# A delta-rule chain with paired outputs, per-head increments, one masked scan and a column moved to ScalarE

## The chip, the cores and the metric

The program runs on one core of a Trainium2 chip. TensorE (PE) multiplies matrices, with its weight loads shown apart (PEld); VectorE (DVE), ScalarE (ACT) and GpSimd (POOL) work on tiles; SyncE (SP) issues the DMAs. Each engine takes its instructions in the order of its own queue and waits where an operand is not ready. The metric is the device time of one execution in microseconds, smaller being better.

## The reference

A decoder block on a sequence of 2048 tokens of width 1024 with two token mixers side by side, a convolution branch and an RWKV-7 branch. What the change touches is the second:

```python
    decay = jnp.exp(-jnp.exp(-jax.nn.softplus(-w_pre) - 0.5))
    ...
    def step(state, inp):
        r_t, w_t, k_t, v_t, kk_t, b_t = inp
        sk = jnp.einsum('bhvk,bhk->bhv', state, kk_t)
        state = (state * w_t[:, :, None, :] - sk[..., None] * b_t[:, :, None, :]
                 + v_t[..., None] * k_t[:, :, None, :])
        return state, jnp.einsum('bhvk,bhk->bhv', state, r_t)
```

There are 16 heads with a state of 64 by 64 each. Ahead of it, `_token_shift(z, mu)` forms `z + mu * (prev - z)` with the preceding token's row for `r`, `k`, `v` and two low-rank inputs. Around it stand one input projection from 1024 to 9344 columns, two branch output projections, a final projection and norms. Everything is computed in float32 accuracy: the projections split each operand into two reduced parts (`hi`, `lo`) and add three products.

## The kernel before

The sequence is cut into four blocks of 512 tokens (`TB`), and a block into eight chunks of 64 (`CH`, `NCH`). Features lie on the partitions. A block's input projection is a series of tiles of 128 features (`project`, `mm3`): eight feature tiles times three products, 24 matmuls of 512 columns at L179. While these run, the scheduler places between them the steps of generators that work on the recurrence: the generator's `yield a, b` says that the step takes about `a` us of TensorE and that the next is due `b` us later on a virtual clock, which each projection step moves on (`tick`, `poll`). The queues' final order comes from a scheduler that knows priorities; `tc.high_priority(HP)` lifts what is in it, and the convolution's taps (L890, 29 a tile plus a first and a last one, on VectorE) have a low one, so that they fill VectorE's queue.

**Token shift.** `shifted` (L466 to L474) gets a projection tile in PSUM. ScalarE forms `t1 = (1 - mu) * ps` (L468), VectorE adds `mu` times the columns one to the left for columns 1 to 511 (L470), then does the first column from the saved last column of the block before (`carry`, L472), then saves the new last column (L474). There are 25 such tiles a block.

**Pairs.** `pair` prepares two heads (128 features) of a block: 32 pairs in all. It makes the log-decay `M` by a tanh (L516), adds one to each column and sums along each chunk with eight scans of 64 columns (L524, `initial=0`, `one` the added ones), takes exponentials of the sums (L527, L529), and from `k` and `r` the tiles `BK` and `KR`; squares of `k` are summed over a head at L551, the chunk matrices come from `KR` and `BK` at L587, `tk` are transposes of `BK` (L607).

**Groups.** `group` takes two pairs (four heads) of a block: 16 groups, one after the other. It inverts the chunk matrices (POOL L671 and L673, PE L718 and L722) and then runs the chain over the eight chunks with the state `Sg` (two pairs `q`, two heads `hh` each, one head on partitions 0 to 63 and the other on 64 to 127). Two PSUM buffers `xo[0]` and `xo[1]` serve even and odd chunks. One chunk `c`, with `e = c % 2`:

- L775: state times `KR` into `xo[e][:, 0:2]`; ScalarE makes `Se` from the state (L779), VectorE `Xz` (L780).
- L784: the corrected values, on the half of `xo[e]`'s partitions that `prow(e)` names. Between its matmuls, one by one, stand those of the next chunk, L749, into the other buffer and the other half. After them come the outputs of the chunk before (`olast(c - 1)`, L758: four products of 64 columns on the half `vrow`). ScalarE copies `Xz` for the next chunk (L753) and the outputs (`ocopy`, L762); VectorE scales the values into `uv` (L795).
- L800: the state's increment, `tk` times `uv`, for both heads of a pair in one product of 128 by 128 of which the two diagonal blocks are used, into `xo[e][:, 2:4]`. VectorE updates the state in four instructions, one a head (L804).

After the last chunk come its outputs alone, then a group norm, and 30 us later on the virtual clock the transposes at L839. An fp32 matmul stands in the profile as two instructions. Tiles of PSUM come round from pools; a write into `xo` waits for what still reads or writes that buffer.

Of the kernel before, what the change touches and what calls it, by code (L numbers as in the profile page):

```python
# [9 lines left out]
F32 = mybir.dt.float32  # L10
F32R = mybir.dt.float32r
I32 = mybir.dt.int32
AF = mybir.ActivationFunctionType
ALU = mybir.AluOpType
# [4 lines left out]
P = 128  # L19
D = 1024  # L20
KT = D // P
TB = 512
NTT = TB // P
CH = 64
NCH = TB // CH
# [5 lines left out]
BKB, T2B, OCB = 1, 2, 2  # L31
KRB, TKB, ASB = 4, 4, 4
HP = 3000
# [33 lines left out]
def hybrid_block(ctx: ExitStack, tc: tile.TileContext, x, vecs, convk, w2a2, final_g, ada, w_in, w_co, w_ro, w_o, crow, out,  # L67
                 seq=2048, groups=(0, 1, 2, 3), phase2=True, dbg=None):
    nc = tc.nc
# [199 lines left out]
    c1 = late.enter_context(tc.tile_pool(name="c1", bufs=1))  # L269
    l3 = late.enter_context(tc.tile_pool(name="l3", bufs=3))  # L270
    lt = late.enter_context(tc.tile_pool(name="lt", bufs=2))
# [18 lines left out]
    nc.vector.tensor_scalar(out=hlb, in0=vc("conv_ln_b"), scalar1=0.5, scalar2=None, op0=ALU.mult)  # L290

    bones = c1.tile([P, P], F32R, name="bones")
    bf = lt.tile([P, P], F32, name="bf", tag="X", bufs=1)
    nc.vector.memset(bf, 0.0)
    nc.vector.memset(bf[0:64, 0:64], 1.0)
    nc.vector.memset(bf[64:128, 64:128], 1.0)
# [7 lines left out]

    Xz = c1.tile([P, 2, 2, P], F32, name="Xz")
    nc.gpsimd.memset(Xz, 0.0)
    one = c1.tile([P, CH], F32, name="one")
    nc.vector.memset(one, 1.0)
    maskA = c1.tile([P, 4, CH], F32, name="maskA")
    m64 = lt.tile([64, 2, CH], F32, name="m64", tag="X", bufs=1)  # L310
    nc.gpsimd.memset(m64, 1.0)
    for i, base in ((0, 0), (1, -1)):
        nc.gpsimd.affine_select(out=m64[:, i, :], in_=m64[:, i, :], compare_op=ALU.is_ge, fill=0.0, base=base,
# [10 lines left out]
    mu1 = dcol("mu1", "rwkv_mu", -1.0, 1.0)  # L324
# [13 lines left out]
    carry = c1.tile([P, 25], F32, name="carry")  # L338
# [126 lines left out]
    def shifted(ps, ti, dst):  # L465
        mi = ti - T_R  # L466
        t1 = e2.tile([P, TB], F32, name="t1", tag="t2", bufs=T2B)
        nc.scalar.activation(t1, ps, AF.Identity, scale=mu1[:, mi:mi + 1])  # L468
        mu = vc("rwkv_mu", mi)
        nc.vector.scalar_tensor_tensor(out=dst[:, 1:], in0=ps[:, 0:TB - 1], scalar=mu, in1=t1[:, 1:],  # L470
                                       op0=ALU.mult, op1=ALU.add)
        nc.vector.scalar_tensor_tensor(out=dst[:, 0:1], in0=carry[:, mi:mi + 1], scalar=mu, in1=t1[:, 0:1],  # L472
                                       op0=ALU.mult, op1=ALU.add)
        lastv[0] = nc.vector.tensor_copy(carry[:, mi:mi + 1], ps[:, TB - 1:TB])  # L474

    def ch3(ap):
        return ap.rearrange("p (c t) -> p c t", t=CH)
# [10 lines left out]
    def vrow(e):  # L488
        return slice(0, 64) if e == 0 else slice(64, 128)

    kcol, rcol = prow, vrow
# [9 lines left out]
    def pair(G, q_, box):  # L501
        b, pr, lora, uv, Asb, rn = G.b, 2 * G.g + q_, G.lora, G.uv, G.As[q_], G.rn
# [12 lines left out]
        M = e1.tile([P, TB], F32, name="M", tag="M")  # L515
# [3 lines left out]
        nc.tensor.matmul(pq, wlo[:, 1, :], lora[1], start=False, stop=True)  # L519
        ta = e1.tile([P, TB], F32, name="ta", tag="ta", bufs=1)  # L520
        nc.scalar.activation(ta, pq, AF.Tanh, scale=0.5, bias=a0h[:, pr:pr + 1])
        for c in range(NCH):
            cs = slice(c * CH, c * CH + CH)
            nc.vector.tensor_tensor_scan(out=M[:, cs], data0=one, data1=M[:, cs], initial=0.0, op0=ALU.add, op1=ALU.add)  # L524
        E1 = e1.tile([P, NCH, CH + 1], F32, name="E1", tag="E1", bufs=1)
        nc.gpsimd.memset(E1[:, :, 0:1], 1.0)
        nc.scalar.activation(E1[:, :, 1:], ch3(M), AF.Exp, scale=-DECAY)  # L527
# [16 lines left out]
        for e in range(2):  # L544
            nc.vector.scalar_tensor_tensor(out=KR[:, :, CH * (1 + e):CH * (2 + e)], in0=k4[:, :, e, :],
                                           scalar=vc("rwkv_k_k", pr), in1=E1x[:, :, e, :], op0=ALU.mult, op1=ALU.mult)
# [3 lines left out]
        for c in range(NCH):  # L550
            nc.tensor.matmul(pss[prow(c % 2), c // 2, :], sq[:, c * CH:c * CH + CH], hones, start=True, stop=True,  # L551
                             skip_group_check=True)
# [6 lines left out]
                                       scalar=hkk[:, pr:pr + 1], in1=E2.rearrange("p (c n) -> p c n", n=2 * CH),  # L559
                                       op0=ALU.mult, op1=ALU.mult)  # L560
# [18 lines left out]
        for c4 in range(NCH // 4):  # L579
            yield free  # L580
            pA = [pa.tile([P, 2, 256], F32, name="aux", tag="aux") for _ in range(2)]
            for c in range(4):
                cc, e = (c4 * 4 + c) // 2, c % 2
                es = slice(e * 128, e * 128 + 128)
                for hh in range(2):
                    hs = slice(64 * hh, 64 * hh + 64)
                    nc.tensor.matmul(pA[hh][:, c // 2, es], BK[hs, cc, es], KR[hs, cc, es],  # L587
                                     start=(c == 0), stop=(c == 3), skip_group_check=True)
            for hh in range(2):
                nc.vector.tensor_tensor(  # L590
                    out=Asb[:, hh, c4 * 4:c4 * 4 + 4, :].rearrange("p (a e) n -> p a (e n)", e=2),
                    in0=pA[hh], in1=flat(maskA).unsqueeze(1).broadcast_to([P, 2, 256]), op=ALU.mult)
# [8 lines left out]
        tk = l3.tile([P, NCH, P], F32, name="tk", tag="tk", bufs=TKB)  # L601
        for c4 in range(NCH // 4):
            yield free
            pt = pa.tile([P, 4, P], F32, name="aux", tag="aux")
            for c in range(4):
                cc, e = (c4 * 4 + c) // 2, c % 2
# [36 lines left out]
    lastv = [None]  # L643

    def group(G, before):
# [94 lines left out]
        O = uv[:, 0::2]  # L740
# [12 lines left out]
            nc.scalar.copy(Xz[prow(c % 2), c % 2], xo[c % 2][prow(c % 2), 2:4])  # L753

        def olast(c):
            vr, rc = vrow(c % 2), rcol(c % 2)
            for n, (q, hh, hs) in enumerate(every):
                nc.tensor.matmul(xo[c % 2][vr, q, hs], As[q][:, hh, c, rc], uv[:, c, q, hs],  # L758
                                 start=False, stop=(n == 3), skip_group_check=True)

        def ocopy(c):
            nc.scalar.copy(O[vrow(c % 2), c // 2], xo[c % 2][vrow(c % 2), 0:2])  # L762

        for n in range(4):
            xval(0, n)
# [3 lines left out]
        for c in range(NCH):  # L769
            cc, e = c // 2, c % 2  # L770
            pr_, b_ = prow(e), xo[e]
            es = slice(e * 128, e * 128 + 128)
            Se = lt.tile([P, 2, P], F32, name="Se", tag="Se", bufs=1)
            for q in range(2):
                nc.tensor.matmul(b_[:, q, :], R[q]["KR"][:, cc, es], Sg[:, q, :], start=(q == 0), stop=False,  # L775
                                 skip_group_check=True)
            with tc.high_priority(HP):
                for q in range(2):
                    nc.scalar.mul(Se[:, q, :], Sg[:, q, :], R[q]["pe"][:, c:c + 1])  # L779
                nc.vector.tensor_tensor(out=Xz[pr_, e], in0=b_[pr_, 0:2], in1=Xz[pr_, e], op=ALU.add)  # L780
            yield 0.6, 2.6

            for n, (q, hh, hs) in enumerate(every):
                nc.tensor.matmul(b_[pr_, q, hs], As[q][:, hh, c, kcol(e)], Xz[:, e, q, hs],  # L784
                                 start=(n == 0), stop=(n == 3), skip_group_check=True)
                if c + 1 < NCH:
                    xval(c + 1, n)
            if c:
                olast(c - 1)
            with tc.high_priority(HP):  # L790
                if c + 1 < NCH:
                    xcopy(c + 1)
                if c:
                    ocopy(c - 1)
                nc.vector.tensor_tensor(out=uv[pr_, c].rearrange("p q (h n) -> p q h n", n=64),  # L795
                                        in0=b_[pr_, 0:2].rearrange("p q (h n) -> p q h n", n=64),
                                        in1=rn[pr_, :, cc, :].unsqueeze(3).broadcast_to([64, 2, 2, 64]), op=ALU.mult)
            yield 1.1, 2.5
            for q in range(2):
                nc.tensor.matmul(b_[:, 2 + q, :], R[q]["tk"][:, c, :], uv[:, c, q, :], start=False, stop=(q == 1),  # L800
                                 skip_group_check=True)
            with tc.high_priority(HP):
                for q, hh, hs in every:
                    nc.vector.scalar_tensor_tensor(out=Sg[hs, q, hs], in0=b_[hs, 2 + q, hs],  # L804
                                                   scalar=R[q]["pe"][hs, c:c + 1], in1=Se[hs, q, hs],
                                                   op0=ALU.mult, op1=ALU.add)
            yield 0.6, 3.3
        olast(NCH - 1)
        ocopy(NCH - 1)

        O16 = O.rearrange("p a q (h n) -> p a (q h) n", n=64)
        st = lt.tile([P, 16], F32, name="gst", tag="gst")
# [505 lines left out]
```

## Time and profile before

| | us |
|---|---|
| median of 3 runs | 3033.8 (3033.46 to 3036.6) |
| the profiled execution | 3034.01 |
| its span, first to last instruction | 3032.2 |
| TensorE clock granted, mean share | 0.969 |

How the span divides: until 60 us the first tiles and the input norm are prepared; the four blocks' projections with the chain between them last until about 2440, and the last group's chain until about 2560 beside the output projections, which end the program. In these stretches TensorE's busy share and the others' are:

| us | PE | DVE | ACT | POOL |
|---|---|---|---|---|
| 60 to 760 | 634.45 | 524.85 | 274.77 | 333.48 |
| 760 to 1360 | 556.98 | 434.83 | 203.79 | 289.22 |
| 1360 to 1960 | 567.57 | 437.24 | 197.61 | 307.56 |
| 1960 to 2440 | 459.05 | 348.77 | 147.55 | 234.31 |

In the views below, a row of the timeline is start in us, length in us, engine, line, operation, tiles, shape and count; its length is from start to modelled end, and since matmuls overlap in the array, the distance of starts says what one costs. A row of the waits is who waited, for whom, total us, times, longest. A row of the groups by line gives busy time, mean ns of one instruction, and the idle time of the engine ahead of it.

### The profile page before, as it was taken

How to read it: one execution, taken by the hardware profiler on the slowest of the kernel's cores; microseconds unless marked ns; L12 is line 12 of the kernel's file. 1: busy time of each engine (PE TensorE's matmuls, PEld its weight loads, DVE VectorE, ACT ScalarE, POOL GpSimd, SP SyncE). 2: the span in 40 equal slices, each digit the busy share in tenths (PEclk: the TensorE clock that was granted, in tenths of full speed). 3: DMA queues.
4: the chain of work that ended last, by engine and by line, in shares of the span. 5: the costliest groups of instructions: out<-in, count | busy, mean ns of one | idle time of the engine just before them, and what ended most of it. 6: DMA issues, size and time to landing. Idle time of an engine off the chain costs nothing. (4 is left out here: it accounts for less than half of the span.)

```text
span 3032.2 us, 51026 instructions
## 1 busy us (share of the span) xinstructions
PE 2817.1 (93%) x18640; PEld 2297.6 (76%) x18640; DVE 2072.0 (68%) x4160; ACT 1001.3 (33%) x1936; POOL 1229.8 (41%) x1790
## 2 busy tenths in 40 slices
PE   6889798999799999999999999999999999899998
PEld 5767686777687777777878777778787778788988
DVE  6867777779676778676767777666778755753433
ACT  4424343434233324242423242323323323421211
POOL 3464637352536355425373655253644500400000
PEclk9989899999899999999999999999999999999999
DMA  8677657686757666857676668565656666976665
GB/s 309 234 247 249 217 204 257 204 268 197 241 187 258 198 203 218 284 173 240 191 257 203 210 217 305 168 208 171 193 184 213 237 210 195 336 250 222 215 222 174
DMA packets 363146, 680.00 MB, mean 224 GB/s; under 512 B 135632, under 2 KB 154384, under 8 KB 362896
## 3 DMA queue, kind: packets, MB, share of 16 engines
q1 hardware_dynamic: 362896, 676.75, 67.0%
q8 instruction: 147, 2.41, 0.3%
q14 instruction: 103, 0.84, 0.1%
HBM read 494.08 MB, written 181.41 MB: 223 GB/s over the span
## 5 line engine op out<-in xcount | busy, mean ns | idle before, releaser
L179 PE MATMUL ps_main<-h_hi,w_hi 128*128 128x512 f32 x2304 | 970.6, 421 | 19.7 <-DMA w_hi<-kh_in 15.1
L179 PE MATMUL ps_main<-h_hi,w_lo 128*128 128x512 f32 x2304 | 918.6, 399 | 7.2 <-POOL w_lo L164 4.0
L179 PE MATMUL ps_main<-h_lo,w_hi 128*128 128x512 f32 x2304 | 915.4, 397 | 1.3 <-DVE h_lo L397 1.1
L890 DVE SCALAR_TENSOR_TENSOR acc<-u,ck,acc 128x512 f32<-128x512 f32 x928 | 696.7, 751 | 15.9
L179 PEld LDWEIGHTS ps_main<-h_hi,w_hi 128*128 128x128 f32 x2304 | 442.9, 192 | 115.5 <-issue 9.9
L179 PEld LDWEIGHTS ps_main<-h_hi,w_lo 128*128 128x128 f32 x2304 | 440.7, 191 | 114.4 <-POOL w_lo L164 6.2
L179 PEld LDWEIGHTS ps_main<-h_lo,w_hi 128*128 128x128 f32 x2304 | 443.6, 193 | 81.6 <-DVE h_lo L397 2.9
L804 DVE SCALAR_TENSOR_TENSOR S<-xo,pe,Se 64x64 f32<-64x64 f32 x512 | 144.5, 282 | 140.1 <-PE xo L800 130.5
L671 POOL TENSOR_TENSOR itmp<-La,TT 128x126 f32<-128x126 f32 (+22 forms) x496 | 179.8, 363 | 130.2 <-DMA La<-dA 85.2
L162 ACT CAST w_hi<-w_st 128x1024 fp32r<-128x1024 f32 x103 | 108.1, 1049 | 301.4 <-DMA w_st<-w_co_t 124.8
L673 POOL TENSOR_TENSOR TT<-TT,itmp 128x126 f32<-128x126 f32 (+22 forms) x496 | 191.3, 386 | 36.8
L164 POOL TENSOR_TENSOR w_lo<-w_st,w_hi 128x1024 fp32r<-128x1024 f32 x50 | 120.4, 2408 | 131.2 <-ACT w_hi L162 67.3
L779 ACT ACTIVATE Se<-S,pe 128x128 f32<-128x128 f32 x256 | 88.9, 394 | 169.5 <-DVE S L804 169.4
L164 DVE TENSOR_TENSOR w_lo<-w_st,w_hi 128x1024 fp32r<-128x1024 f32 x53 | 65.6, 1238 | 97.2 <-PE ps_main L179 54.8
L795 DVE TENSOR_TENSOR uv<-xo,rn 64x256 f32<-64x256 f32 x128 | 53.6, 419 | 111.4 <-PE xo L784 99.3
L784 PEld LDWEIGHTS xo<-Xz,As 128*64 128x64 f32 x1024 | 70.0, 138 | 68.8 <-DVE Xz L780 32.0
L753 ACT COPY Xz<-xo 64x256 f32<-64x256 f32 x128 | 47.0, 367 | 211.9 <-PE xo L758 141.7
L780 DVE TENSOR_TENSOR Xz<-xo,Xz 64x256 f32<-64x256 f32 x128 | 53.5, 418 | 86.0 <-PE xo L775 78.9
L845 POOL TENSOR_TENSOR oc<-oc,zt 128x512 f32<-128x512 f32 x64 | 81.7, 1285 | 66.6 <-ACT oc L841 39.6
L784 PE MATMUL xo<-Xz,As 128*64 128x64 f32 x1024 | 87.9, 230 | 20.9 <-DVE Xz L780 20.8
L590 DVE TENSOR_TENSOR As<-aux,maskA 128x512 f32<-128x512 f32 x128 | 83.0, 682 | 30.9 <-PE aux L587 30.4
L587 PE MATMUL aux<-KR,BK 64*128 64x128 f32 x1024 | 82.2, 291 | 17.8 <-DVE As L590 9.3
(299 smaller groups left out, 5493.7 us busy)
## 6 DMA issues: line engine op xcount, KB each, us to landing
w_hi<-kh_in SPq DMA_DIRECT2D x219, 512.0 KB, 4.2
w_lo<-kl_in SPq DMA_DIRECT2D x219, 512.0 KB, 5.3
w_st<-w_in_t SPq DMA_DIRECT2D x73, 512.0 KB, 4.5
kh_in<-w_hi SPq DMA_DIRECT2D x71, 512.0 KB, 2.9
kl_in<-w_lo SPq DMA_DIRECT2D x71, 512.0 KB, 3.6
lny<-y_d SPq DMA_DIRECT2D x72, 256.0 KB, 4.4
w_hi<-kh_ro SPq DMA_DIRECT2D x32, 512.0 KB, 3.9
w_lo<-kl_ro SPq DMA_DIRECT2D x32, 512.0 KB, 5.3
```

Of the source, the lines that this page charges most:

```text
L162: nc.scalar.copy(hi, st)
L164: lo_eng.tensor_tensor(out=lo, in0=st, in1=hi.bitcast(F32), op=ALU.subtract)
L179: nc.tensor.matmul(ps[:, qs], ww[:, k, :], aa[k][:, qs], start=(k == 0 and t == 0 and q == 0), stop=(k == KT - 1 and t == 2 and q == ms - ...
L587: nc.tensor.matmul(pA[hh][:, c // 2, es], BK[hs, cc, es], KR[hs, cc, es], start=(c == 0), stop=(c == 3), skip_group_check=True)
L590: nc.vector.tensor_tensor(out=Asb[:, hh, c4 * 4:c4 * 4 + 4, :].rearrange("p (a e) n -> p a (e n)", e=2), in0=pA[hh], in1=flat(maskA).unsqu ...
L671: nc.gpsimd.tensor_tensor(out=tmp[:, :ni, :nt], in0=La[:, j:j + 1, j + 1:].broadcast_to([P, ni, nt]), in1=TT[:, :ni, j:j + 1].broadcast_to ...
L673: nc.gpsimd.tensor_tensor(out=TT[:, :ni, j + 1:], in0=TT[:, :ni, j + 1:], in1=tmp[:, :ni, :nt], op=ALU.add)
L779: nc.scalar.mul(Se[:, q, :], Sg[:, q, :], R[q]["pe"][:, c:c + 1])
L784: nc.tensor.matmul(b_[pr_, q, hs], As[q][:, hh, c, kcol(e)], Xz[:, e, q, hs], start=(n == 0), stop=(n == 3), skip_group_check=True)
L804: nc.vector.scalar_tensor_tensor(out=Sg[hs, q, hs], in0=b_[hs, 2 + q, hs], scalar=R[q]["pe"][hs, c:c + 1], in1=Se[hs, q, hs], op0=ALU.mult ...
L845: nc.gpsimd.tensor_tensor(out=oc, in0=oc, in1=zt, op=op)
L890: nc.vector.scalar_tensor_tensor(out=acc if i + 1 < HALO else yj, in0=u[:, i:i + TB], scalar=ck[:, j, i:i + 1], in1=acc, op0=ALU.mult, op1 ...
```

## The change

Four edits, and two small tiles that move to another buffer.

- Outputs of two chunks by turns: `olast` is called once after each odd chunk, for that chunk and the one before, its matmuls alternating between `xo[0]` and `xo[1]`, and with it ScalarE's two copies. The step after the odd chunk's state update is due after 2.0 instead of 3.3, then comes the output step with 0.5 and 1.5.
- State increment per head by turns: four products of 64 by 64 columns instead of two of 128 by 128, into columns 0 to 63 of `xo[e][:, 2 + q]`, on the partitions of the head.
- Decay sums: ScalarE adds one to all of `M`, then one scan of 512 columns multiplies the running sum by `keep` (ones, and zero at each chunk's first column) and adds `M`.
- Token shift: ScalarE forms the first column from the projection's first column, with `carry` as bias, and the new `carry` as `mu` times the last column.

```diff
-    bf = lt.tile([P, P], F32, name="bf", tag="X", bufs=1)
+    bf = lt.tile([P, P], F32, name="bf", tag="oc", bufs=OCB)
...
-    one = c1.tile([P, CH], F32, name="one")
-    nc.vector.memset(one, 1.0)
+    one1 = c1.tile([P, 1], F32, name="one1")
+    nc.vector.memset(one1, 1.0)
+    keep = c1.tile([P, TB], F32, name="keep")
+    nc.vector.memset(keep, 1.0)
+    nc.vector.memset(keep[:, 0::CH], 0.0)
...
-    m64 = lt.tile([64, 2, CH], F32, name="m64", tag="X", bufs=1)
+    m64 = lt.tile([64, 2, CH], F32, name="m64", tag="oc", bufs=OCB)
...
-        nc.vector.scalar_tensor_tensor(out=dst[:, 1:], in0=ps[:, 0:TB - 1], scalar=mu, in1=t1[:, 1:],
+        nc.scalar.activation(dst[:, 0:1], ps[:, 0:1], AF.Identity, scale=mu1[:, mi:mi + 1], bias=carry[:, mi:mi + 1])
+        nc.scalar.activation(carry[:, mi:mi + 1], ps[:, TB - 1:TB], AF.Identity, scale=mu)
+        lastv[0] = nc.vector.scalar_tensor_tensor(out=dst[:, 1:], in0=ps[:, 0:TB - 1], scalar=mu, in1=t1[:, 1:],
                                        op0=ALU.mult, op1=ALU.add)
-        nc.vector.scalar_tensor_tensor(out=dst[:, 0:1], in0=carry[:, mi:mi + 1], scalar=mu, in1=t1[:, 0:1],
-                                       op0=ALU.mult, op1=ALU.add)
-        lastv[0] = nc.vector.tensor_copy(carry[:, mi:mi + 1], ps[:, TB - 1:TB])
...
-        for c in range(NCH):
-            cs = slice(c * CH, c * CH + CH)
-            nc.vector.tensor_tensor_scan(out=M[:, cs], data0=one, data1=M[:, cs], initial=0.0, op0=ALU.add, op1=ALU.add)
+        nc.scalar.activation(M, M, AF.Identity, bias=one1[:, 0:1])
+        nc.vector.tensor_tensor_scan(out=M, data0=keep, data1=M, initial=0.0, op0=ALU.mult, op1=ALU.add)
...
         def olast(c):
-            vr, rc = vrow(c % 2), rcol(c % 2)
             for n, (q, hh, hs) in enumerate(every):
-                nc.tensor.matmul(xo[c % 2][vr, q, hs], As[q][:, hh, c, rc], uv[:, c, q, hs],
-                                 start=False, stop=(n == 3), skip_group_check=True)
-
-        def ocopy(c):
-            nc.scalar.copy(O[vrow(c % 2), c // 2], xo[c % 2][vrow(c % 2), 0:2])
+                for e in range(2):
+                    nc.tensor.matmul(xo[e][vrow(e), q, hs], As[q][:, hh, c + e, rcol(e)], uv[:, c + e, q, hs],
+                                     start=False, stop=(n == 3), skip_group_check=True)
+            with tc.high_priority(HP):
+                for e in range(2):
+                    nc.scalar.copy(O[vrow(e), c // 2], xo[e][vrow(e), 0:2])
...
-            if c:
-                olast(c - 1)
...
-                if c:
-                    ocopy(c - 1)
...
-            for q in range(2):
-                nc.tensor.matmul(b_[:, 2 + q, :], R[q]["tk"][:, c, :], uv[:, c, q, :], start=False, stop=(q == 1),
-                                 skip_group_check=True)
+            for q, hh, hs in every:
+                nc.tensor.matmul(b_[hs, 2 + q, 0:64], R[q]["tk"][:, c, hs], uv[:, c, q, hs], start=False,
+                                 stop=(q + hh == 2), skip_group_check=True)
...
-                    nc.vector.scalar_tensor_tensor(out=Sg[hs, q, hs], in0=b_[hs, 2 + q, hs],
+                    nc.vector.scalar_tensor_tensor(out=Sg[hs, q, hs], in0=b_[hs, 2 + q, 0:64],
...
-            yield 0.6, 3.3
-        olast(NCH - 1)
-        ocopy(NCH - 1)
+            yield 0.6, 2.0 if e else 3.3
+            if e:
+                olast(c - 1)
+                yield 0.5, 1.5
```

In the changed kernel the lines are numbered L776 (was L775), L781 (L780), L785 (L784), L750 (L749), L759 (L758), L792 (L795), L797 (L800), L801 (L804), L525 (L524).

## The prediction, made before the changed kernel ran

> **What bounds the kernel now.** I read the page first, then the list of who waits for whom on TensorE, then the timeline of TensorE around single visits of the chain.
>
> ```profile
> span 3032.2 us, 51026 instructions
> ...
> PE 2817.1 (93%) x18640; PEld 2297.6 (76%) x18640; DVE 2072.0 (68%) x4160; ACT 1001.3 (33%) x1936; POOL 1229.8 (41%) x1790
> ```
>
> TensorE is busy for 93% of the span and no other engine comes near it. So the end moves by two things alone: time in which TensorE's queue is occupied, and time in which the instruction at its head waits. The chain itself is not the bound: between its steps the queue holds 9 to 15 projection matmuls (L179), and a step that gets longer costs nothing while they cover it. The waits of the chain (L775 to L804) and of the pair work that feeds it (L551, L587, L718, L722) are these:
>
> ```profile
> PE xo L784 <- DVE Xz L780: 20.8, 14, 3.8
> ...
> PE aux L587 <- DVE As L590: 9.3, 7, 4.5
> PE late L722 <- DVE Qs L728: 9.1, 8, 1.9
> PE late L718 <- DVE T L705: 7.9, 2, 4.6
> PE aux L587 <- POOL KR L570: 7.8, 6, 2.8
> PE xo L758 <- DVE S L804: 7.5, 3, 4.4
> PE aux L551 <- ACT sq L543: 5.6, 3, 3.1
> ...
> PE xo L775 <- ACT Xz L753: 2.7, 2, 2.4
> ```
>
> Columns: total us, times, longest. Without L758 and the last row they come to 20.8 + 9.3 + 9.1 + 7.9 + 7.8 + 5.6 = 60.5 us, nearly all released by VectorE, directly or through what it feeds. That is what a lighter VectorE can give back.
>
> **What one visit of TensorE costs.** Projection matmuls start 0.23 us apart. A visit's price is the time from the last projection matmul before it to the second one after it, less two such steps (0.46).
>
> ```profile
> 282.41 0.40 PE L179 MATMUL ps_main<-h_hi,w_lo 128*128 128x512 f32 x1
> ...
> 283.25 0.63 PE L758 MATMUL xo<-uv,As 128*64 128x64 f32 x8
> ...
> 284.15 0.40 PE L179 MATMUL ps_main<-h_lo,w_hi 128*128 128x512 f32 x1
> ```
> ```profile
> 286.45 0.39 PE L179 MATMUL ps_main<-h_hi,w_lo 128*128 128x512 f32 x1
> 286.68 0.60 PE L800 MATMUL xo<-uv,tk 128*128 128x128 f32 x4
> ...
> 287.36 0.40 PE L179 MATMUL ps_main<-h_lo,w_hi 128*128 128x512 f32 x1
> ```
> ```profile
> 325.77 0.40 PE L179 MATMUL ps_main<-h_hi,w_lo 128*128 128x512 f32 x1
> 326.09 0.68 PE L758 MATMUL xo<-uv,As 128*64 128x64 f32 x8
> ...
> 327.04 0.39 PE L179 MATMUL ps_main<-h_lo,w_hi 128*128 128x512 f32 x1
> ```
> ```profile
> 372.39 0.40 PE L179 MATMUL ps_main<-h_hi,w_lo 128*128 128x512 f32 x1
> ...
> 372.94 0.22 PE L749 MATMUL xo<-uv,As 128*64 128x64 f32 x1
> ...
> 373.18 0.22 PE L749 MATMUL xo<-uv,As 128*64 128x64 f32 x1
> ...
> 373.67 0.40 PE L179 MATMUL ps_main<-h_lo,w_hi 128*128 128x512 f32 x1
> ```
>
> An fp32 matmul is two instructions here. In the same order: the mixed visit (16 of L784 and L749, then 8 of L758) costs 284.15 - 282.41 - 0.46 = 1.28 us; the increment L800 (4, of 128 columns) 0.45; the group's last outputs L758 alone (8) 0.81; 16 of L784 and L749 by turns 0.82. So 16 by turns cost what 8 on one half of the columns cost. And half of those 16 would save only 373.18 - 372.94 = 0.24, that is 0.58 us: most of a visit of 64-column tiles is a fixed price of entering and leaving, which the 128-column L800 does not pay.
>
> **Outputs by turns.** Each of the 16 groups now pays the mixed visit in seven of its eight steps, in the eighth with an L784 that has no L749 beside it (priced as 8 on one half, 0.81), and the last visit. The outputs' part is 6 x (1.28 - 0.82) + (1.28 - 0.81) + 0.81 = 4.04 us. After: four visits of 16 by turns, 4 x 0.82 = 3.28. Saved: 0.76 us a group, 12 us in all.
>
> **Increment per head.** Eight instructions of 64 columns in place of four of 128: 0.58 - 0.45 = 0.13 us more where the visit stands alone. In the built order 82 of the 128 do: +10.7 us. The other 46 stand beside transposes (L607), the KR-BK products (L587) or the like, and share one price of entering with them or pay a second one. The mixed visit shows the first (L758 behind L749 adds its 8 starts alone); if each shared all of it, they would save about as much as the 82 lose, if none, they add 6. I take nothing. Outputs and increments together: -12 + 11 = -1 us, with -10 to +5 as bounds. What is saved by turns goes back into entering and leaving more often.
>
> The Trainium skill, in TensorEngine Tiling, Key Properties, says that a change of tiling mode, not merely of tile, drains TensorE. The visits above agree (0.58 against 0.45). By that rule taken strictly, a neighbour of another tile size such as L587 would share nothing, and the two edits would come to about +5 rather than -1.
>
> **Scan.** Columns: busy us, mean ns, then idle time before.
>
> ```profile
> L890 DVE SCALAR_TENSOR_TENSOR acc<-u,ck,acc 128x512 f32<-128x512 f32 x928 | 696.7, 751 | 15.9
> L524 DVE TENSOR_TENSOR_SCAN M<-one,M 128x64 f32<-128x64 f32 x256 | 90.9, 420 | 8.4 <-ACT M L516 8.1
> L474 DVE COPY carry<-ps_main 128x1 f32<-128x1 f32 x96 | 14.4, 150 | 1.5
> L472 DVE SCALAR_TENSOR_TENSOR r<-carry,v,t 128x1 f32<-128x1 f32 x32 | 13.6, 424 | 0.0
> L472 DVE SCALAR_TENSOR_TENSOR vv<-carry,v,t 128x1 f32<-128x1 f32 x32 | 11.3, 353 | 0.0
> L472 DVE SCALAR_TENSOR_TENSOR k<-carry,v,t 128x1 f32<-128x1 f32 x32 | 10.0, 312 | 0.0
> L516 ACT ACTIVATE M<-aux,w0h 128x512 f32<-128x512 f32 x32 | 21.9, 685 | 7.7 <-PE aux L514 7.5
> L779 ACT ACTIVATE Se<-S,pe 128x128 f32<-128x128 f32 x256 | 88.9, 394 | 169.5 <-DVE S L804 169.4
> ```
> ```profile
> 240.88 1.95 DVE L524 TENSOR_TENSOR_SCAN M<-one,M 128x64 f32<-128x64 f32 x8
> ```
>
> A pair's eight scans hold VectorE for 90.9 / 32 = 2.8 us on the mean, 1.95 when nothing interferes. One scan of 512 columns is bounded by the plain 512-column tap below (0.75) and by the eight back to back above (1.95); I take 1.3, between. VectorE is spared 32 x (2.8 - 1.3) = 48 us. ScalarE gains 32 activations like L516, 22 us, and each pair's exponentials wait for it, so they start 2.8 - 1.3 - 0.7 = 0.8 us sooner.
>
> The Trainium skill, in DVE: opcode table, instruction layouts, handler registers and perf-mode slots, section 6, says that the built-in scan runs at half throughput because of its feedback; by that, 512 columns would cost about two taps, an estimate of 1.5 us, and the sum would change by 6 us of VectorE time alone.
>
> **First column.** L472 and L474 leave VectorE: 13.6 + 11.3 + 10.0 + 14.4 = 49 us. Two ScalarE instructions of one column take their place, 200 in all, each under L779's 0.39 us: at most 79 us on an engine that is busy a third of the time. They stand behind the activation that already reads the same projection; k, r and vv are ready 0.3 to 0.4 us sooner, since the column runs beside the 511-column instruction.
>
> So VectorE loses 48 + 49 = 97 of 2072 us. In the built order the usual number of taps (L890) ahead of a state update falls from four to three. Of the 60.5 us of waits I take a third back, 20 us: more than the tap in four, since the blocks of eight scans in the update's way go too. The bounds are nothing and half (30).
>
> **New waits.** The outputs of an odd step's two chunks are written into the buffer that this step's state update (L804, four instructions) is reading, so the visit waits for the update; behind it in TensorE's queue wait all projections. Before, only the last of a group's eight had this, behind 15 projection matmuls, and 3 of 16 were late, for 7.5 us together (quoted above). Now all 64 have it, behind 9: the cover shrinks by 6 x 0.23 = 1.4 us, so these three add 4. For the other 48, one odd step as it is now:
>
> ```profile
> 1027.92 0.60 PE L800 MATMUL xo<-uv,tk 128*128 128x128 f32 x4
> ```
> ```profile
> 1028.22 0.75 DVE L470 SCALAR_TENSOR_TENSOR k<-ps_main,v,t 128x511 f32<-128x511 f32 x1
> 1028.89 0.21 DVE L472 SCALAR_TENSOR_TENSOR k<-carry,v,t 128x1 f32<-128x1 f32 x1
> 1029.01 0.75 DVE L890 SCALAR_TENSOR_TENSOR acc<-u,ck,acc 128x512 f32<-128x512 f32 x1
> 1029.67 1.19 DVE L804 SCALAR_TENSOR_TENSOR S<-xo,pe,Se 64x64 f32<-64x64 f32 x4
> ```
>
> The update ends at 1030.86, 2.94 us after the increment's start; the new cover from there is about 0.24 + 0.15 + 8 x 0.23 + 0.32 = 2.5 us (the visit's own starts, the way out at 373.18 to 373.33, eight steps, the way in). Late by 0.45. Bounds for the 48: nothing, and 48 x 0.45 = 22. I take 5, since one such step has its L472 in front, which goes, and usually a tap fewer. Together +9, up to 26. Also, three times a group the next even step's L775 must wait for ScalarE's copy of these outputs, six projection matmuls earlier. The nearest row is L775 behind L753: 2.7 us in two waits, 1.35 each. I take 2, at most six such waits, 8.
>
> **Sum.** -1 + 9 + 2 - 20 = -10 us against the profiled execution's own 3034.0 (its span and 1.8 around it; the median of the runs is 3033.8): **3024 us**.
>
> **Rivals.**
> *Nothing moves.* VectorE's saved time falls into its idle third; a tenth of the waits comes back (6) and the new ones cost 6: about 3033. For it: many of these waits hang on a DMA or a weight split further back. Against: L784's wait for L780 is VectorE's own queue.
> *Slower: outputs behind the state update.* Place: the output visit of an odd step. It decides once these waits pass 19 us, where they eat the whole sum: 4 for the three late ones and 0.45 in 33 of the other 48. Price at the upper bound, with a third of the hoped return (7): 26 + 2 - 1 - 7 = +20, 3054. For it: the odd step above. Against: the scans that hold VectorE for 1.95 us in one piece become one shorter piece.
> *It doesn't do what it says.* L797's halves write one PSUM buffer, L784 and L749 two; were the turns not to overlap there, eight starts at L758's pace, 0.81 against 0.45 a visit, cost 0.36 x 82 = 30 us: 3054 with the other terms. Against it: L551, which writes one buffer with alternate halves, makes 16 starts in a visit like the one of L784 and L749:
>
> ```profile
> 730.25 0.40 PE L179 MATMUL ps_main<-h_hi,w_lo 128*128 128x512 f32 x1
> 730.57 0.63 PE L551 MATMUL aux<-bones,sq 128*64 128x2 f32 x16
> ...
> 731.48 0.39 PE L179 MATMUL ps_main<-h_lo,w_hi 128*128 128x512 f32 x1
> ```
>
> **How the numbers follow.** Forecast 0.46, nothing moves 0.19, outputs behind the update 0.28, no overlap 0.07. A difference under 0.2% (6 us) cannot be told from none. Faster 0.46, same 0.19, slower 0.35. The forecast's own range is 2999 (half the old waits back, the three late ones and a tenth of the 48 the only new ones: -1 + 6 - 30 = -25, and 10 for the visits' bound) to 3028. To hold 8 in 10 the range takes in both slower cases: 2999 to 3056.
>
> **What would show it.** A visit of eight L797 alone at 0.58 us, of 16 L759 at 0.82; L525 at 1.3 us; VectorE's busy time near 1975; L784's wait for Xz and L587's waits down by a third; L759's wait for S near 9 us. I am wrong if L759's waits pass 20 us, if L797's visits cost 0.8, or if the old waits stay although VectorE is lighter.

## The result and the profile after

The changed kernel takes 3042.0 us (median of 13 runs), the one before 3033.8 (13 runs): ratio 1.0028, 95% interval 1.0019 to 1.0037. It is slower by 8 us; 3024 had been forecast. The profiled executions have spans of 3039.8 and 3032.2.

The page of the changed kernel, first part:

```profile
span 3039.8 us, 51701 instructions
...
PE 2803.5 (92%) x19152; PEld 2237.3 (74%) x19152; DVE 2003.5 (66%) x3738; ACT 1066.8 (35%) x2168; POOL 1243.1 (41%) x1790
```

TensorE's span is its busy time and its idle time. Busy fell from 2817.1 to 2803.5, by 13.6 us; idle rose from 215.1 to 236.3, by 21.2. The difference is the 7.6 us by which the span grew: TensorE has less to do and waits longer. Where it waits, in the list of TensorE's waits (total us, times, longest):

```profile
PE xo L797 <- DVE uv L792: 16.3, 16, 2.8
PE ps_main L179 <- DVE mr L1142: 16.1, 4, 13.6
...
PE late L719 <- DVE T L706: 14.4, 4, 8.1
...
PE aux L588 <- POOL KR L571: 10.9, 7, 3.1
PE xo L785 <- DVE Xz L781: 10.7, 11, 1.6
PE xo L759 <- DVE S L801: 9.8, 8, 4.5
PE late L723 <- DVE Qs L729: 8.2, 5, 2.2
PE aux L719 <- DVE T L706: 8.1, 5, 3.6
...
PE aux L588 <- DVE As L591: 4.0, 4, 3.0
...
PE aux L552 <- ACT sq L544: 3.2, 1, 3.2
...
PE xo L776 <- ACT uv L763: 2.5, 3, 1.2
```

The same list of the kernel before, rows that the prediction does not show:

```profile
PE ps_main L179 <- DVE mr L1144: 9.8, 5, 6.5
...
PE aux L718 <- DVE T L705: 2.9, 3, 1.2
...
PE xo L800 <- DVE uv L795: 1.9, 3, 0.8
```

Two waits are new in size: the increment's wait for `uv` (16.3 for 1.9), and the projection matmuls' wait for `mr`, whose longest went from 6.5 to 13.6. The second is a single wait in one place. To find it, the span is cut at two projection matmuls that are the same in every kernel, the 7,393rd and the 7,585th L179: between them lies the work behind the last group (the last layer norm and the first projections behind it). The windows' columns are the stretch, its length, TensorE's busy time and count, granted clock, DMA share, GB/s. Before:

```profile
0.00:2607.20 2607.20, 2412.94 (x16335) 0.97 0.67 224
2607.20:2662.60 55.40, 47.31 (x195) 0.94 0.88 305
```

After:

```profile
0.00:2603.90 2603.90, 2397.87 (x16845) 0.97 0.67 223
2603.90:2670.40 66.50, 48.65 (x196) 0.85 0.80 283
```

Up to the last layer norm the change is 3.3 us ahead in these two executions: 15.1 less busy, 11.8 more idle. Then 11.1 us are lost in 66.5. In the timelines, columns as in the prediction's, the last entry is the idle time ahead and who ended it. TensorE, before:

```profile
2618.17 1.02 PE L1189 MATMUL pvar<-qs,ones 128*128 128x512 f32 x2
2625.73 0.79 PE L179 MATMUL ps_main<-m_hi,w_hi 128*128 128x512 f32 x1 [6.54 <-DVE mr L1144]
```

VectorE, before:

```profile
2624.40 0.68 DVE L1191 TENSOR_SCALAR ve<-pvar 128x512 f32<-128x512 f32 x1
2625.00 0.67 DVE L1144 SCALAR_TENSOR_TENSOR mr<-rth,ps_main 128x512 f32<-128x512 f32 x1
```

TensorE, after:

```profile
2618.95 2.07 PE L1187 MATMUL pvar<-qs,ones 128*128 128x512 f32 x2 [3.52 <-POOL qs L1185]
2634.64 0.79 PE L179 MATMUL ps_main<-m_hi,w_hi 128*128 128x512 f32 x1 [13.62 <-DVE mr L1142]
```

VectorE, after:

```profile
2622.86 5.38 DVE L1256 SCALAR_TENSOR_TENSOR xt<-xt,rs,fg 128x512 f32<-128x512 f32 x8
2628.16 0.68 DVE L1099 TENSOR_TENSOR o_lo<-zt,o_hi 128x512 fp32r<-128x512 f32 x1
2628.76 0.68 DVE L1189 TENSOR_SCALAR ve<-pvar 128x512 f32<-128x512 f32 x1
...
2632.70 1.28 DVE L1099 TENSOR_TENSOR o_lo<-zt,o_hi 128x512 fp32r<-128x512 f32 x2
2633.91 0.68 DVE L1142 SCALAR_TENSOR_TENSOR mr<-rth,ps_main 128x512 f32<-128x512 f32 x1
```

The rows of VectorE follow each other without idle time in both. It frees the PSUM buffer for which TensorE waits (`mr`) right behind `ve` before the change; after it, up to 0.6 us a piece, three steps of the reciprocal root and five splits of `o_lo` come between (rows left out above). Counted from the start of the second window, `pvar` starts 4.0 us later than before (3.5 of them a wait for `qs`), `ve` 7.6 and `mr` 12.1. Both orders compute the same; the queue was laid out anew, in a place that no line of the diff names.

### The profile page after: what moved, and what is told of

Its sections match the earlier page's. It is cut to its first block, busy times and chain, and to the rows that moved or that the text cites. A ratio compares the mean times of both kernels' runs of the same rounds, so it can differ in the third digit from the quotient of the medians.

```text
span 3039.8 us, 51701 instructions
## 1 busy us (share of the span) xinstructions
PE 2803.5 (92%) x19152; PEld 2237.3 (74%) x19152; DVE 2003.5 (66%) x3738; ACT 1066.8 (35%) x2168; POOL 1243.1 (41%) x1790
## 5 line engine op out<-in xcount | busy, mean ns | idle before, releaser
L179 PE MATMUL ps_main<-h_hi,w_hi 128*128 128x512 f32 x2304 | 971.9, 422 | 11.3 <-DMA w_hi<-kh_in 6.5
L179 PE MATMUL ps_main<-h_hi,w_lo 128*128 128x512 f32 x2304 | 917.8, 398 | 18.0 <-DMA w_lo<-kl_in 11.2
L179 PE MATMUL ps_main<-h_lo,w_hi 128*128 128x512 f32 x2304 | 912.4, 396 | 0.2
L179 PEld LDWEIGHTS ps_main<-h_hi,w_lo 128*128 128x128 f32 x2304 | 439.6, 191 | 126.0 <-DMA w_lo<-kl_in 13.8
L179 PEld LDWEIGHTS ps_main<-h_hi,w_hi 128*128 128x128 f32 x2304 | 440.9, 191 | 111.8 <-DMA w_hi<-kh_in 6.9
L179 PEld LDWEIGHTS ps_main<-h_lo,w_hi 128*128 128x128 f32 x2304 | 441.7, 192 | 78.6 <-DVE h_lo L400 1.1
L801 DVE SCALAR_TENSOR_TENSOR S<-xo,pe,Se 64x64 f32<-64x64 f32 x512 | 144.7, 283 | 142.9 <-PE xo L797 133.8
L781 DVE TENSOR_TENSOR Xz<-xo,Xz 64x256 f32<-64x256 f32 x128 | 53.7, 420 | 152.9 <-PE xo L776 148.2
L780 ACT ACTIVATE Se<-S,pe 128x128 f32<-128x128 f32 x256 | 88.9, 394 | 186.6 <-DVE S L801 183.8
L627 POOL TENSOR_TENSOR vv<-rk,vv 128x512 f32<-128x512 f32 x32 | 41.4, 1295 | 205.0 <-PE aux L624 154.0
L754 ACT COPY Xz<-xo 64x256 f32<-64x256 f32 x128 | 46.9, 366 | 202.9 <-PE xo L750 201.9
L792 DVE TENSOR_TENSOR uv<-xo,rn 64x256 f32<-64x256 f32 x128 | 53.8, 420 | 93.4 <-PE xo L750 59.0
L785 PEld LDWEIGHTS xo<-Xz,As 128*64 128x64 f32 x1024 | 69.2, 137 | 57.5 <-issue 30.5
L588 PE MATMUL aux<-KR,BK 64*128 64x128 f32 x1024 | 82.0, 295 | 16.9 <-POOL KR L571 10.9
```

Of the source, the lines that this page charges most:

```text
L179: nc.tensor.matmul(ps[:, qs], ww[:, k, :], aa[k][:, qs], start=(k == 0 and t == 0 and q == 0), stop=(k == KT - 1 and t == 2 and q == ms - ...
```

## The experiments

Each kernel ran in rounds with the kernel before; a ratio is to that, with its 95% interval. "Stretch" and "tail" are the two windows above, read from the one execution that was profiled. e3 and e12 are the same kernel, and their stretches are 12 us apart, TensorE's busy time 8 us (2806.9 and 2814.8): a stretch carries that much scatter, while the tail is 55.4 in both. So the ratios decide, and a stretch only hints.

| label | edits in it | ratio | stretch | tail |
|---|---|---|---|---|
| before | | 1 | 2607.2 | 55.4 |
| after | all | 1.0028 [1.0019, 1.0037] | 2603.9 | 66.5 |
| e1 | outputs | 1.0034 [1.0019, 1.0049] | 2605.7 | 65.9 |
| e2 | increments | 1.0009 [0.9996, 1.0022] | 2599.7 | 55.4 |
| e7 | scan | 0.997 [0.9959, 0.9982] | 2595.6 | 55.4 |
| e8 | column | 1.0007 [0.9994, 1.002] | 2604.5 | 55.4 |
| e3 | scan, column | 0.9933 [0.9915, 0.995] | 2582.4 | 55.4 |
| e12 | scan, column | 0.9951 [0.9934, 0.9969] | 2594.6 | 55.4 |
| e5 | increments, scan, column | 0.998 [0.9967, 0.9994] | 2605.6 | 55.4 |
| e6 | scan, column, outputs in blocks 0 to 2 | 0.9978 [0.9966, 0.9989] | 2601.3 | 55.4 |
| e4 | all, outputs in blocks 0 to 2 alone | 1.0019 [1.0006, 1.0033] | 2613.5 | 55.4 |
| e10 | outputs in the last group alone | 1.0014 [1.0002, 1.0026] | 2601.3 | 61.5 |

### One part alone, and the edit kept out of the last block

e1, e2 and e3 are the hunks of the diff by themselves. e4 is the whole change with the following against the kernel before, where `TURNS2(b, g)` returns `b < 3`:

```diff
+        turns2 = TURNS2(b, g)
...
-            if c:
+            if c and not turns2:
                 olast(c - 1)
...
+            if e and turns2:
+                olast2(c - 1)
```

Here `olast2` is the changed `olast`, and `olast` that of before.

> The kernel before with the outputs by turns alone. Theory T (the loss sits behind the last group: the new place of the outputs in block 3 changes the order of VectorE's queue while the last layer norm and the output projections run, and the evacuation that frees the projections' PSUM comes behind more operand splits): the wait of a projection for mr at about 2630 us is near 13.6 us instead of 6.5, progress at the last projection is about 10 us behind what it was at 2600, and the time is 1.002 to 1.004 of before although TensorE's visits save 12 us. Theory C (the loss is in the chain: 64-column increments that cost 0.14 us more a visit, and new waits for uv and for the state): without the increments and with VectorE as loaded as before, the time is between 0.997 and 1.001, and the tail as before.

> The kernel before with the state increment per head alone. Both theories have the visits at 0.60 us against 0.46, 82 of which stand alone: +11 us, 1.003 to 1.004, with the tail as before. Theory C adds waits in the chain (L800 for uv): 1.004 to 1.007. If the visits' price lies beside waits that were there anyway: 1.000 to 1.001.

> The kernel before with the masked scan and the first column on ScalarE, the chain as before. Both theories let VectorE lose some 80 to 100 us of busy time. If a third of the waits that VectorE ends come back as the prediction had it: 20 us, 0.993 to 0.995. If VectorE's time was cover, as the rival had it: 0.998 to 1.001.

> The changed kernel, but with the outputs by turns in blocks 0 to 2 alone; the four groups of block 3 have the old place of the outputs. VectorE's queue behind the last group then stands in the order of before. Theory T: the wait for mr near 2630 us is back at 6 to 7 us, the time falls by 8 to 10 us from the changed kernel's, to 0.999 to 1.001 of before. Theory C: a quarter of the outputs' share is undone, the time stays at 1.002 to 1.004.

The windows of the outputs alone:

```profile
0.00:2605.70 2605.70, 2399.18 (x16333) 0.97 0.67 223
2605.70:2671.60 65.90, 48.70 (x196) 0.84 0.82 285
```

and of the change with blocks 0 to 2 alone by turns:

```profile
0.00:2613.50 2613.50, 2410.73 (x16847) 0.97 0.68 223
2613.50:2668.90 55.40, 47.30 (x195) 0.94 0.88 308
```

In the profiled execution the outputs alone save 13.8 us of busy time, and the stretch is 1.5 us shorter: 12 us came back as idle time. The tail then costs 10.5 us more, as in the whole change; with block 3 as before it is 55.4 again, and the longest wait for `mr` 6.5. So, with this due time, the long tail belongs to the outputs by turns in block 3. It isn't the whole loss: the fourth kernel keeps its short tail and is still slower than before, by 1.0019. Theory T had it 8 to 10 us faster than the change; by the ratios it is 3 us faster, with intervals that overlap. The increments alone (1.0009) can't be told from nothing: the 11 us that their dearer visits were to cost don't show. And scan and column alone are worth 20 us, far more than the change has left of them.

### What the chain takes from scan and column

> Everything of the change but the outputs by turns. Known on this job's scale: scan and column alone 0.9933 of the kernel before (-20 us), increments alone 1.0009 (+3). Theory I (what eats the gain is the dearer increment visit, 0.60 for 0.46 us, 75 of them alone between projections: +11 us, and its cost is seen whole once VectorE is early): 3012 + 11 = 3023, ratio 0.9968 or more. Theory O (the outputs in the chain eat it, because without the old output visit the increments arrive at uv 0.46 us earlier than VectorE has it): the increments alone take at most the 3 us they take by themselves: 3015, ratio 0.994; the wait of the increments for uv stays at 8 to 10 us as in scan and column alone.

> Scan and column, and the outputs by turns in blocks 0 to 2 alone; the increments stay as before. Theory O: nearly all of the 20 us is eaten here, 3030 to 3035, ratio 1.000 to 1.002, with the increments' wait for uv at 14 us or more. Theory I: the gain stays, 3012 to 3016, ratio 0.993 to 0.9945. Theory B (only both edits of the chain together eat it): this run and the one with increments, scan and column both stay under 3020.

> Decay sums as one masked scan, and nothing else. VectorE has 8 scans of 0.26 us (2.1 us) less and one of 1.545 us more per pair of heads, 32 times: -0.55 us x 32 = -18 us of VectorE. Theory S (the sums stand ahead of everything in a group, so what they give back counts whole): most of the 20 us, 3015 to 3020, ratio 0.995. Theory L (the column edit, four VectorE columns and four copies per 512 tokens, counts as well and by its 79 us of VectorE more): -4 us, ratio 0.9985.

> The shifted projection's first column on ScalarE, and nothing else: two one-column instructions less on VectorE for each of 96 shifted projections, two of 0.34 and 0.26 us more on ScalarE, and the 511 column instruction now waits for them. Theory L: -16 us, 3015, ratio 0.9945. Theory S: -4 us or nothing, ratio 0.9985 to 1.0. If both single runs are near 1.0, the 20 us need both.

With scan and column in all four, the ratio goes from 0.9933 to 0.998 with the increments, to 0.9978 with the outputs in blocks 0 to 2, and to 1.0019 with both. Each seems to take about 14 us, and both together about 26, so neither theory of a single culprit holds, nor the one that needs both. But the scan alone gives 9 us and the column alone costs 2, which do not add up to 20. Repeated later (e12), scan and column gave 15, and by that the two prices would be 8 to 9 us.

### The tail by itself

e10 has the old outputs everywhere but in the last group (`TURNS2(b, g)` returns `(b, g) == (3, 3)`), and no other edit.

> Outputs by turns in the last group of block 3 alone, all else as before. Theory T (the edit puts VectorE's evacuations behind the reciprocal root and the splits in the queue behind the last group): the whole 10 us with a sixteenth of the edit, 3041, ratio 1.003, the wait for mr at 14 us or more. If the loss of the outputs alone (1.0034) came from the chain in all 16 groups: under 1 us here, ratio 1.000.

```profile
0.00:2601.30 2601.30, 2411.15 (x16333) 0.97 0.67 224
2601.30:2662.80 61.50, 48.53 (x197) 0.86 0.81 282
```

One sixteenth of the edit makes the tail 6.1 us longer, and the kernel slower by 4 us. The longest wait for `mr` is 10.4 us, between the two seen so far. The mechanism holds, the forecast 10 us does not.

### Room before the increment

The largest new wait in the chain is the increment's for `uv`. The output visit that stood between Xz's visit and the increment is gone, so TensorE arrives sooner. These kernels let the increment's step be due later:

```diff
-            yield 1.1, 2.5
+            yield 1.1, 3.4
```

In the whole change 15 projection matmuls then stand between the two steps in 55 of the 128 chunks, and never more than 12 without it.

> The whole change, with the step of the state increment due 3.4 instead of 2.5 after the step that makes uv: in the queue 15 instead of 12 matmuls (229 ns each) stand between the two in half the chunks. Theory W (the new wait for uv, 16.3 us in the changed kernel, is lost time): that wait falls under 5 us and the stretch up to the last layer norm becomes 8 to 12 us shorter than its 2603.9. Theory V (the chain through VectorE sets the pace, and a wait taken away there comes back at the next one: state, T, KR): the wait falls as well, but the stretch stays within 4 us of 2603.9. Both: in the built queue two of VectorE's first evacuations of the projection behind the last group stand ahead of the reciprocal root again, so the stretch there should be near 55 us instead of 66.5. In all 3020 for W, 3028 to 3032 for V.

> Scan and column alone, with the increment's step due 3.4 instead of 2.5 after uv. Scan and column alone had 8.1 us of waits of the increment for uv. Theory W: most of these go, 3005, ratio 0.991. Theory V: 3010 to 3014, ratio 0.993, as without it.

> Scan and column once more, as the yardstick of this job: 3012, ratio 0.9933. Were the first five executions a lucky draw, it would stand near the sum of the single runs, 3024, ratio 0.998.

> Scan and column, outputs by turns in blocks 0 to 2, old increments, and the increment's step due 3.4 after uv. Theory P (the outputs' loss in the chain is the work that they took from between Xz and uv, so room there gives it back): the stretch up to the last layer norm falls by 15 to 20 us from the 2601.3 of the same kernel without room, to 2581 to 2586; in all 3010, ratio 0.993. Theory V (the room moves the waits to Xz and to GpSimd's uv, as it did with scan and column alone, 2598.3 for 2594.6): 2600 or more, 3030, ratio 1.000.

> Increments per head, scan and column, outputs as before, and the increment's step due 3.4 after uv. Theory P: the old output visit still stands between Xz and uv, so the room is too much here as it was without the increments: not shorter than the 2605.6 of the same kernel without room, 3036 to 3045, ratio 1.002 or more. Theory I (it is the increments that come back through room): 2590 or less, 3015, ratio 0.995.

> The change with the old increments in all blocks, and the increment's step due 3.4 after uv. Theory P: as the whole change with room (3019, stretch 2580.1), less the 8 to 11 us that the increments per head cost: 3008 to 3011, ratio 0.992, stretch near 2570. Were the increments free: 3019, ratio 0.996.

| label | edits, all with due 3.4 | ratio | the same with 2.5 |
|---|---|---|---|
| e9 | all | 0.9959 [0.9943, 0.9975] | 1.0028 |
| e11 | scan, column | 1.0021 [1.001, 1.0032] | 0.9933, 0.9951 |
| e13 | scan, column, outputs in blocks 0 to 2 | 1.0054 [1.0038, 1.007] | 0.9978 |
| e14 | increments, scan, column | 1.0033 [1.002, 1.0046] | 0.998 |
| e15 | scan, column, outputs | 1.0069 [1.0055, 1.0083] | not run |

Room made the whole change 21 us faster by its ratio, to 3019.3 us, which beats the kernel before. Taken alone this would have passed for proof that the new wait is the loss. But the same room made the three other kernels that ran both ways 16 to 27 us slower: e13 and e15 were to show the loss of the outputs paid back, at 3010 us, and took 3046.8 and 3051.5. That theory fell, though e14, at 3041.0, came out within its 3036 to 3045. Scan and column alone with room were put at 3005 or 3010 to 3014 and took 3036.0. TensorE's waits in the whole change with room:

```profile
PE late L837 <- POOL uv L829: 46.9, 14, 13.6
PE xo L785 <- DVE Xz L781: 20.9, 14, 4.7
...
PE ps_main L179 <- DVE mr L1142: 8.0, 3, 6.1
```

and in e15, without the increments:

```profile
PE late L837 <- POOL uv L829: 65.1, 14, 20.7
PE xo L785 <- DVE Xz L781: 23.8, 18, 4.0
```

The wait for `uv` is gone from the larger rows of both. In its place the wait for Xz doubles (10.7 in the changed kernel), and the one at L837 for GpSimd grows from

```profile
PE late L837 <- POOL uv L829: 18.2, 2, 14.8
```

in the changed kernel to 46.9 and 65.1. It is 46 to 65 us in all five kernels with this room. So waits do move to later steps; that the whole change wins on balance and the others lose isn't explained by the room. The tail, expected near 55 us with this due time, is 60.9 to 68.4 in all five, 61.8 and 61.7 without any output by turns (e11, e14): it follows the order that a build gives, and the outputs are only one thing that can change that order.

### The same edit with other due times

> The whole change with the increment's step due 2.6 instead of 2.5 after uv: next to nothing by intent (12 matmuls of room in 90 instead of 80 of 128 chunks, and the late evacuations behind the last group stay), but the built queues differ from the changed kernel's in a fifth of VectorE's rows. Theory R (the room sets the time): 3038 to 3042, ratio 1.002 to 1.0028. Theory L (where the scheduler happens to put VectorE's tails and taps weighs as much as the edits): more than 0.3% away from 1.0028, to either side.

> The whole change with the increment's step due 2.8 after uv: 15 matmuls of room in 60 of 128 chunks, as with 3.4 (55 chunks), but 9 in 44 (with 3.4 in 6). Theory R: between the changed kernel and the one with 3.4 and nearer to that: 3022 to 3030, ratio 0.997 to 1.000, the wait for uv under 8 us. Theory L: no order among 2.5, 2.8, 3.1 and 3.4; 3.4 was one draw, and this lies anywhere from 3015 to 3050.

> The whole change with the increment's step due 3.1 after uv: 15 matmuls of room in 51 of 128 chunks, 9 in 23. Theory R: between the one with 2.8 and the one with 3.4: 3019 to 3026, ratio 0.996 to 0.9985. Theory L: anywhere from 3015 to 3050.

The whole change by the second number of that `yield`:

| due after uv | ratio to before | stretch | tail |
|---|---|---|---|
| 2.5 (the change) | 1.0028 [1.0019, 1.0037] | 2603.9 | 66.5 |
| 2.6 (e16) | 0.9995 [0.9986, 1.0004] | 2598.0 | 66.1 |
| 2.8 (e17) | 1.0024 [1.0015, 1.0034] | 2603.1 | 62.5 |
| 3.1 (e18) | 1.0038 [1.0024, 1.0052] | 2604.2 | 65.8 |
| 3.4 (e9) | 0.9959 [0.9943, 0.9975] | 2580.1 | 64.5 |

What the room does inside, in the same order (matmuls that stand between the two steps, mean of 128 chunks; then TensorE's waits, total us):

| due after uv | matmuls | increment for `uv` | Xz | L837 for GpSimd |
|---|---|---|---|---|
| 2.5 | 10.7 | 16.3 | 10.7 | 18.2 |
| 2.6 | 11.1 | 7.3 | 11.1 | 17.9 |
| 2.8 | 12.3 | 5.5 | 10.8 | 35.5 |
| 3.1 | 12.5 | 1.8 | 21.9 | 51.2 |
| 3.4 | 13.0 | 0.2 | 20.9 | 46.9 |

The waits follow the room, the time does not. A tenth of a microsecond in a due time, which changes next to nothing in TensorE's room, is worth 10 us (1.0028 to 0.9995, intervals apart), and the neighbours 3.1 and 3.4 differ by 24. The kernel with 3.4 waits 23 us longer in these three columns together than the change and is 21 us faster. The mean of the five ratios is 1.0009, their standard deviation 0.0032, that is 10 us. So room by itself does not set the time. What else differs from build to build is where the scheduler puts taps, splits and evacuations in the queues; that this is the cause is argued and was not traced. The intervals show that each kernel's time is steady; the scatter lies between builds.

Part of it goes along with the clock that was granted to TensorE. On the mean of the runs it is 0.968 for the kernel before in every round here, 0.972 and 0.971 with scan and column (e3, e12), 0.963 in e13 and e15. A thousandth of clock is worth at most 3 us (an estimate: 0.001 of the 3032 us, were TensorE busy throughout), so at most 12 of the 20 us that e3 gains, and at most 17 us in e13 and e15, which lose 16 and 21. It does not sort the five due times: 3.1 and 3.4 stand at 0.968 and 0.969. Nor does it explain the change, which has 0.969 and is slower. Whether this clock is a cause or only follows the waits was not tested; the last section shows what one wait does to it.

## Why the prediction was wrong

**Single visits were priced rightly.** In the changed kernel, by the same measure as before:

```profile
287.24 0.39 PE L179 MATMUL ps_main<-h_lo,w_hi 128*128 128x512 f32 x1
287.46 0.40 PE L179 MATMUL ps_main<-h_hi,w_lo 128*128 128x512 f32 x1
287.79 0.45 PE L797 MATMUL xo<-uv,tk 128*64 128x64 f32 x8
288.17 0.50 PE L179 MATMUL ps_main<-h_hi,w_hi 128*128 128x512 f32 x1
288.51 0.40 PE L179 MATMUL ps_main<-h_lo,w_hi 128*128 128x512 f32 x1
```

288.51 - 287.46 - 0.46 = 0.59 us for eight L797, forecast 0.58.

```profile
300.94 0.40 PE L179 MATMUL ps_main<-h_hi,w_lo 128*128 128x512 f32 x1
301.27 0.69 PE L759 MATMUL xo<-uv,As 128*64 128x64 f32 x16
...
302.23 0.40 PE L179 MATMUL ps_main<-h_lo,w_hi 128*128 128x512 f32 x1
```

302.23 - 300.94 - 0.46 = 0.83 for sixteen L759, forecast 0.82. The turns do overlap in one PSUM buffer, so that rival is out. The sum of all visits, -1 us with -10 to +5 as bounds, was not measured: TensorE's busy time fell by 13.6, but two executions of one kernel (e3, e12) differ in it by 8.

**The new waits that were named were sized rightly or too high.** L759's wait for the state is 9.8 us, forecast near 9; but the prediction's sum put 9 on top of the 7.5 that L758 already had, and the added part is 2.3. L776's wait for the copies is 2.5, forecast 2. The rival of outputs behind the state update needed 19.

**The scan was a little dearer than taken.** The groups of VectorE's and ScalarE's instructions by line, after (busy us, mean ns, then idle time before); VectorE:

```profile
L525 DVE TENSOR_TENSOR_SCAN M<-keep,M 128x512 f32<-128x512 f32 x32 | 49.4, 1545 | 10.8 <-ACT M L524 10.6
```

ScalarE:

```profile
L474 ACT ACTIVATE carry<-ps_main,v 128x1 f32<-128x1 f32 x96 | 25.1, 262 | 2.7
L524 ACT ACTIVATE M<-M,one 128x512 f32<-128x512 f32 x32 | 23.2, 726 | 0.0
```

1.545 us a scan for the 1.3 taken. That is the 1.5 which the prediction worked out from the Trainium skill (DVE: opcode table, instruction layouts, handler registers and perf-mode slots, section 6); page and trace agree. VectorE is busy 2003.5 us, 68.5 less, where 97 less was forecast. The dearer scan is 8 us of the difference. The rest is in how the 97 was added up: neighbouring rows overlap on VectorE (in the prediction's own rows L472 starts at 1028.89, while L470 lasts until 1028.97), so a line's busy time is more than goes when the line goes. The scan alone (e7) took 22.8 us off VectorE's busy time, where 48 was forecast, and the column alone (e8) 32.0, where 49 was.

**The step that failed** is "of the 60.5 us of waits I take a third back, 20 us", taken together with the sum's silence on what the edits of the chain give up. The six waits it named are now 10.7 + 4.0 + 8.2 + 14.4 + 10.9 + 3.2 = 51.4: 9 us came back and not 20. Even that leaves out a second row of the wait for `T`, at L719, which grew from 2.9 to 8.1; with it 4 us came back. The wait for Xz halved, as hoped; that for `T` went from 10.8 to 22.5 in its two rows. With scan and column alone, 15 to 20 us came off the whole time. Beside the outputs and the increments the relief did not stay:

- The wait of the increment for `uv` was missing from the list of new waits: +14.4 us. The prediction asked for whom the moved output visit would wait; it did not ask what had stood in its old place, and what is due right behind that.
- No term was there for the order of VectorE's queue outside the chain. Behind the last group it cost 11 us, and that with the old due time the outputs in block 3 bring it about is shown by the kernels with and without them there. That is more than the 8 us by which the kernel is slower; yet with the old outputs in block 3 (e4) the time fell by only some 3.
- What the output visits save counted as a gain of the whole 12 us. TensorE's busy time did fall by about that much with the outputs alone, and 12 us of idle time took its place (one execution each).

None of the rivals was this. The range, 2999 to 3056, holds the 3042 only because it was drawn to take in the two slower cases, and neither of these happened: that is luck. What the forecast lacked most was a bound for the build itself: five builds of this change differ by up to 24 us, so a sum of -10 from local prices says little about the sign.

**What stays open.** Which of the reordered instructions decide in the chain was not traced, nor was the granted clock held apart from the waits. The prices of 14 us for increments and outputs on top of scan and column, and the gain of 15 to 20 us of scan and column, are differences of single builds and carry the same scatter of some 10 us. Only the tail's 11 us have a cause that was shown. That the change makes the kernel slower is shown for this build, not for the idea. Scan and column with due 2.5 (3012.4 and 3017.0 us), and the whole change with due 3.4 (3019.3), beat both kernels.

## What to carry to other kernels

Where a scheduler lays out the queues, an edit is two things: its local prices, which can be read off single visits, and a new draw of the order everywhere, which cannot. Before believing in a gain or a loss of a few tenths of a per cent, build the same edit with a due time or priority moved by next to nothing and see how far the time moves. When work is moved out of a place, ask what it was covering there, and look at the stage behind the last step that was touched, not only at the steps themselves.

## What the runs showed of the hardware

A long wait of TensorE costs more than its length in the two cases looked at. After the 13.62 us wait for `mr` the matmuls do not start 0.23 us apart at once:

```profile
2635.23 0.63 PE L179 MATMUL ps_main<-m_lo,w_hi 128*128 128x512 f32 x1
2635.66 0.63 PE L179 MATMUL ps_main<-m_hi,w_lo 128*128 128x512 f32 x1
2636.09 0.63 PE L179 MATMUL ps_main<-m_hi,w_hi 128*128 128x512 f32 x1
```

Counted from the first matmul at 2634.64, the next comes 0.59 later and those behind it 0.43 apart, until 2637.79: 3.15 us for seven steps that else take 1.61. The granted clock in this window is 0.50, and 0.99 in the 7 us behind it. The wait of 6.54 us in the kernel before is followed by the same (4.0 us at a granted clock of 0.50), so it doesn't explain the difference of the two; by these two cases it adds some 1.5 to 2 us to what removing such a wait is worth.

On ScalarE an activation of a single column still takes 262 ns, a third of the 726 ns of 512 columns. That engine is busy for 35% of the span here and has room for them; by itself the move gained nothing (e8, 1.0007).
